# All four sums of a pair's weight blocks made by GpSimd from plain loads

## The chip, the cores and the metric

One core of a Trainium2 chip. Its engines run their own instruction queues side by side: TensorE (PE, multiplies; its weight loads are shown as PEld), VectorE (DVE), ScalarE (ACT), GpSimd (POOL) and SyncE (SP, which issues loads). The metric is the device time of one execution in microseconds. A change of 0.2% (4.5 us) is about what a measurement of this kernel can tell.

## What is computed

A trunk of two layers over 512 tokens of width 1024. Each layer is a half-step SwiGLU, a mixer (attention or convolution), cross attention to a memory and a second half-step SwiGLU. The four SwiGLU blocks are what the change touches:

```python
def swiglu(h, w_in, w_out):
    g, u = split_cols(h @ w_in, (D_FF, D_FF))      # D_FF = 2816
    return (jax.nn.silu(g) * u) @ w_out

x = x + 0.5 * swiglu(rms_norm(x, g[0]), ffn1_w_in[layer], ffn1_w_out[layer])
...
x = x + 0.5 * swiglu(rms_norm(x, g[4]), ffn2_w_in[layer], ffn2_w_out[layer])
```

## The kernel before

All products are fp32 split in two parts, hi and lo (`mm3`: three matmuls for one product). A weight block is loaded (`raw`, or a sum of blocks), ScalarE copies it to the hi part of a tile `w` (in the profile `w<-raw`, `w<-a`, `w<-s`), and VectorE subtracts to get the lo part (the same names on DVE). Six `w` tiles are in use at a time, so splits wait for TensorE to give tiles back.

A feed-forward block has 22 column blocks of 128, done in three parts (`PARTS`: 7, 7 and 8), each followed by its output projection. The first 4 column blocks (5 in the first feed-forward block) are multiplied plainly, with gate and up one after the other. The rest go as *pairs* (`Pair`): the gate block and the up block of one column block, and the two halves of the tokens, are taken as a 2 x 2 block product with seven multiplications in place of eight. The left matrix has the blocks A11 and A12 (`w1`, the gate's columns, first and second half of the contraction: one load of 128 x 1024, tile `raw`, called a1) and A21 and A22 (`w2`, the up columns). Besides A11, A12 and A22 themselves the seven products need four sums of blocks:

- s31, a tile of 1024 columns with A11 + A21 in its left half and A21 + A22 in its right half,
- s2 = A21 + A22 + A11,
- s4 = s2 + A12.

The token side is prepared once a block by VectorE and ScalarE (`Norm.seven`, tiles `hn` and `bop`).

The order of products of a pair on TensorE is: first and second product (from a1), the product with A22 of the pair before it (p4: `w<-a`), the product with s2, the product with s4 of the pair before, and two products from s31, 12 matmuls of 256 columns each. The splits come in the order a1, A22 of the pair before, s2, s4 of the pair before, s31.

Class `Sums` (line 372) makes the sums. `loads` (383) is run through by the loader in the order of the weights: it loads A11 and A22 side by side into a tile of tag P (`s<-ffn_in` on SP), then a1 (`raw<-ffn_in`), then A22 once more by itself (`a<-ffn_in`). `acc` (400) then adds A21 to both halves of the tile by a DMA that accumulates, issued by GpSimd (`s<-ffn_in` on POOL). `add` (406) makes s2 and s4 by two adds on GpSimd (`s<-s,raw`). Buffers: three `raw`, two of tag P, two of tag `ph` (A22), one for s2, two for s4; each has a token that says when it may be used again.

The order on every engine is set ahead of time: tasks are Python generators, and a small planner (`Sched`) with a price for each operation runs the task with the best priority that is ready by its own clock. Its price of the accumulating DMA is 1.04 us and 2.2 us until it is seen; of an add of 512 columns 1.17 us. Waits on tokens come before waits on data, and each engine runs what it is given in order.

Of the kernel before, what the change touches and what calls it, by code (L numbers as in the profile page):

```python
# [9 lines left out]
F32 = mybir.dt.float32  # L10
# [4 lines left out]
ALU = mybir.AluOpType  # L15
# [4 lines left out]
P = 128  # L20
# [27 lines left out]
WMAX = 1024  # L48
# [220 lines left out]
def tile_trunk(ctx: ExitStack, tc: tile.TileContext, a: dict, out: bass.AP, nsteps: int = 8):  # L269
    nc = tc.nc  # L270
    sch = Sched()
    M, SC, TR, OU = ("m", 3), ("s", 2), ("t", 2), ("o", 1)
    pe, act, dve, pool = (Engine(sch, e, n) for e, n in (
        (nc.tensor, "pe"), (nc.scalar, "act"), (nc.vector, "dve"), (nc.gpsimd, "pool")))
    sync, swdge = Engine(sch, nc.sync, "dma"), Engine(sch, nc.gpsimd, "swdge")
# [4 lines left out]
    tp = Pool(sch, ctx.enter_context(tc.tile_pool(name="tmp", bufs=2)), 2)  # L280
# [56 lines left out]
    tok_q, tok_p, tok_pair = Token(2), Token(2), Token(1)  # L337
    tok_slot = Token(9)

    tok_a22, tok_sum = Token(2), Token(2)  # L340


    class Source:


        def __init__(self, tok, uses=1):
            self.tok, self.left = tok, uses
            self.ap, self.ev = None, Event()
# [23 lines left out]
    class Sums:  # L372
# [2 lines left out]


        def __init__(self, w1, w2):
            self.a1 = Chunk(w1, WMAX, 3)
            self.a22, self.s31 = Source(tok_a22), Source(tok_p, 2)
            self.s2, self.s4 = Source(tok_os, 2), Source(tok_sum)  # L380
            self.w1, self.w2 = w1, w2

        def loads(self):
            h = WMAX // 2
            yield tok_p
            t = tp.tile([P, WMAX], F32, tag="P", name="s31")
            t2 = t.rearrange("p (a c) -> p a c", a=2)
            gap = self.w2.offset + h - self.w1.offset
            sync.dma_start(out=t2, in_=bass.AP(self.w1.tensor, self.w1.offset,
                                               [list(self.w1.ap[0]), [gap, 2], [1, h]]))  # L390
            sch.add(self.acc(t, t2), 2)
            yield W.tok_raw
            self.a1.load()
            yield tok_a22
            u = tp.tile([P, h], F32, tag="ph", name="a22")
            sync.dma_start(out=u, in_=self.w2[:, h:])
            self.a22.there(u)
            sch.add(self.add(), 2)

        def acc(self, t, t2):  # L400
            yield Need([t])
            a21 = self.w2[:, :WMAX // 2].unsqueeze(1).to_broadcast([P, 2, WMAX // 2])
            swdge.dma_start(out=t2, in_=a21, accum_op=ALU.add)
            self.s31.there(t)

        def add(self):
            h = WMAX // 2
            yield self.s31.ev
            yield tok_os
            a1, t = self.a1.ap, self.s31.ap  # L410
            yield Need([a1, t])
            s2 = tp.tile([P, h], F32, tag="os", name="s2", bufs=1)
            pool.tensor_tensor(s2, t[:, h:], a1[:, :h], ALU.add)
            self.s31.used()
            self.a1.used()
            self.s2.there(s2)
            yield tok_sum
            s4 = tp.tile([P, h], F32, tag="pl", name="s4")
            pool.tensor_tensor(s4, s2, a1[:, h:], ALU.add)
            self.s2.used()  # L420
            self.a1.used()
            self.s4.there(s4)
# [108 lines left out]
    def token_sums(acc):  # L531

        n = acc.shape[-1] // P
        ps = yield from turn_bank("ss")
        for t in range(n):
            transpose(ps[:, t * P:(t + 1) * P], acc[:, t * P:(t + 1) * P])
        yield Need([ps])
        ss = tp.tile([P, NT], F32, tag="ss", name="ss_c")
        dve.tensor_reduce(ss[:, :n], ps[:, :n * P].rearrange("p (t c) -> p t c", t=n), AX.X, ALU.add)
        tok_t.give()  # L540
        return ss[:, :n]
# [784 lines left out]
    def setup(after):  # L1326
# [79 lines left out]
        for d in range(KD):  # L1406
            raw = tp.tile([P, NMEM], F32, tag="memr", name="mem0")
            swdge.dma_start(out=raw, in_=a["mem"][:, d, :])
            yield Need([raw])
            if d == 0:  # L1410
                act.activation(acc, raw, AF.Square)
            else:
                sq = st[:, 3 + d % 2]
                act.activation(sq, raw, AF.Square)
                yield Need([sq])
                pool.tensor_tensor(acc, acc, sq, ALU.add)
# [621 lines left out]
```

## Time and profile before

| what | us |
|---|---|
| median of 3 runs (2250.31 to 2252.67) | 2251.84 |
| the profiled execution | 2253.21 |
| its span, first to last instruction | 2251.3 |
| TensorE busy | 2213.8 |
| VectorE busy | 1446.7 |
| ScalarE busy | 1073.0 |
| GpSimd busy | 553.3 |
| TensorE's granted clock, mean | 0.998 of full speed |
| read from HBM | 273.18 MB, 123 GB/s over the span |

A row of the order in time has the start, the length, the engine, the source line (nearly always 107, a helper that records every operation), the operation, out<-in, the shape and the count; in brackets stands the engine's idle time before it and what ended it. So instructions are told apart by the names of their tiles. The feed-forward blocks lie at about 9 to 370, 805 to 1158, 1158 to 1511 and 1893 to 2251 us.

### The profile page before, as it was taken

What the parts mean: (1) busy time and instruction counts of PE and PEld (TensorE: products, weight loads), DVE (VectorE), ACT (ScalarE), POOL (GpSimd) and SP (SyncE); (2) the same over time, 40 slices, a digit from 0 to 9 for tenths busy, and PEclk for the clock granted to TensorE, in tenths of its full rate; (3) what the DMA queues carried; (4) which work ended last, traced back from release to release, by engine and by line L of the source; (5) the groups of instructions that cost most, each with busy time, mean ns of one, the idle gap of its engine ahead of it and who ended that gap; (6) DMA issues with size and microseconds to landing.
All of it is one profiled execution on the core that took longest, in us unless ns stands there. A gap on an engine that the chain in (4) does not pass through costs nothing.

```text
span 2251.3 us, 35196 instructions
## 1 busy us (share of the span) xinstructions
PE 2213.8 (98%) x13880; PEld 1979.2 (88%) x13880; DVE 1446.7 (64%) x2302; ACT 1073.0 (48%) x1839; POOL 553.3 (25%) x501
## 2 busy tenths in 40 slices
PE   9998999999999999999999999999999999999999
PEld 7898998889878888999988898989888888889897
DVE  8656565576676686565667474755766667847473
ACT  5344454555565454444544353545544554435352
POOL 1153323432320031313222232323122102213230
PEclk9999999999999999999999999999999999999999
DMA  5455652212332243646534555633123332456562
GB/s 188 117 154 161 166 152 87 75 57 78 102 112 86 93 124 98 171 141 164 147 106 119 153 151 153 170 101 108 58 90 122 98 104 85 131 139 165 144 180 84
DMA packets 106165, 277.59 MB, mean 123 GB/s; under 512 B 11736, under 2 KB 13784, under 8 KB 106000
## 3 DMA queue, kind: packets, MB, share of 16 engines
q1 hardware_dynamic: 83248, 232.63, 31.3%
q0 software_dynamic: 22752, 42.71, 10.8%
q8 instruction: 109, 1.79, 0.3%
q14 instruction: 56, 0.46, 0.1%
HBM read 273.18 MB, written 4.21 MB: 123 GB/s over the span
## 4 chain that ended last, share of the span: by engine, by line
PE 79%; DVE 10%; issue 3%; POOL 3%; DMA 3%; ACT 2%; SPq 0%; POOLq 0%; DVEq 0%; ACTq 0%
PE ps_m L107 44%; PE ps_o L107 27%; DVE w L107 3%; DMA s<-ffn_in 2%; DVE hn L107 2%; PE ps_pv L107 2%; DVE bop L107 2%; PE ps_s L107 1%; PE ps_x L107 1%; PE xo L107 1%; PE ps_pt L107 1%; DVE xl L107 1%; POOL s L107 1%; ACT w L107 1%; POOL qe L107 1%
## 5 line engine op out<-in xcount | busy, mean ns | idle before, releaser
L107 PE MATMUL ps_m<-bop,w 128*128 128x256 f32 x5964 | 728.0, 284 | 17.7 <-DVE g L107 9.2
L107 PEld LDWEIGHTS ps_m<-bop,w 128*128 128x128 f32 x5964 | 722.9, 193 | 23.9 <-DVE g L107 10.2
L107 ACT ACTIVATE w<-raw 128x1024 fp32r<-128x1024 f32 (+2 forms) x332 | 340.4, 1029 | 425.9 <-PE ps_o L107 229.9
L107 DVE TENSOR_TENSOR w<-raw,w 128x1024 fp32r<-128x1024 f32 (+2 forms) x332 | 401.8, 1210 | 148.7 <-ACT w L107 139.2
L107 PE MATMUL ps_m<-xh,w 128*128 128x512 f32 (+1 forms) x1008 | 328.8, 396 | 2.1 <-ACT w L107 2.1
L107 POOL TENSOR_TENSOR s<-s,raw 128x512 f32<-128x512 f32 x142 | 214.5, 1510 | 405.4 <-DMA s<-ffn_in 221.8
L107 PE MATMUL ps_o<-gh,w 128*128 128x512 f32 x944 | 302.5, 389 | 0.0
L107 DVE TENSOR_TENSOR w<-s,w 128x512 fp32r<-128x512 f32 (+1 forms) x213 | 213.7, 1004 | 85.9 <-ACT w L107 57.4
L107 PEld LDWEIGHTS ps_m<-xh,w 128*128 128x128 f32 (+1 forms) x1008 | 188.2, 187 | 44.9 <-ACT w L107 2.7
L107 DVE SCALAR_TENSOR_TENSOR x<-ps_o,x 128x512 f32<-128x512 f32 x160 | 108.6, 687 | 181.5 <-PE ps_o L107 181.2
L107 ACT ACTIVATE w<-s 128x512 fp32r<-128x512 f32 (+1 forms) x213 | 162.5, 767 | 117.6 <-POOL s L107 56.3
L107 PE MATMUL ps_m<-w,xh 128*128 128x256 f32 x1152 | 217.8, 289 | 0.0
L107 PEld LDWEIGHTS ps_o<-gh,w 128*128 128x128 f32 x944 | 177.3, 188 | 36.5
L107 PE MATMUL ps_m<-xl,w 128*128 128x512 f32 (+1 forms) x504 | 197.2, 391 | 0.0
L107 POOL DMA_DIRECT2D s<-ffn_in x71 | 86.1, 1213 | 402.7 <-DMA s<-ffn_in 356.6
L107 PE MATMUL ps_o<-gl,w 128*128 128x512 f32 x472 | 183.8, 389 | 0.0
L107 PEld LDWEIGHTS ps_m<-w,xh 128*128 128x128 f32 x1152 | 178.9, 191 | 1.9 <-issue 1.2
L107 PE MATMUL ps_o<-gated,w 128*128 128x512 f32 x696 | 168.6, 389 | 0.0
L107 PE MATMUL ps_m<-w,xl 128*128 128x256 f32 x576 | 162.7, 282 | 0.0
L107 PEld LDWEIGHTS ps_o<-gated,w 128*128 128x128 f32 x696 | 130.1, 188 | 26.6
L107 POOL TENSOR_TENSOR acc<-acc,sq 128x512 f32<-128x512 f32 x42 | 73.7, 1755 | 246.7 <-ACT sq L107 245.6
L107 PEld LDWEIGHTS ps_m<-xl,w 128*128 128x128 f32 (+1 forms) x504 | 94.5, 187 | 18.7
(453 smaller groups left out, 2812.2 us busy)
## 6 DMA issues: line engine op xcount, KB each, us to landing
raw<-ffn_in SPq DMA_DIRECT2D x103, 512.0 KB, 5.0
s<-ffn_in SPq DMA_DIRECT2D x71, 512.0 KB, 4.3
s<-ffn_in POOLq DMA_DIRECT2D x71, 512.0 KB, 6.0
raw<-ffn_oa SPq DMA_DIRECT2D x64, 448.0 KB, 3.4
a<-ffn_in SPq DMA_DIRECT2D x71, 256.0 KB, 3.8
raw<-ffn_ob SPq DMA_DIRECT2D x32, 512.0 KB, 3.5
raw<-x_kv SPq DMA_DIRECT2D x32, 512.0 KB, 3.4
raw<-even_w SPq DMA_DIRECT2D x24, 512.0 KB, 3.5
```

The lines of the kernel that those rows point to most:

```text
L107: r = fn(*args, **kw)
```

## The change

The accumulating DMA, its task `acc` and the load of A11 and A22 into the tile of s31 are taken out. A21 is loaded by itself, into a buffer of tag `qe` (two of them, used by the attention otherwise), and GpSimd makes all four sums: A21 + A22 into the right half of s31, s2 from it, A21 + A11 into the left half, then s4. The tile of s31 is taken when the adds begin, not when the loads are issued. A22 is now released after the first add and its own split, a1 after three adds and its split.

```diff
@@ class Sums
         def __init__(self, w1, w2):
-            self.a1 = Chunk(w1, WMAX, 3)
-            self.a22, self.s31 = Source(tok_a22), Source(tok_p, 2)
+            self.a1 = Chunk(w1, WMAX, 4)
+            self.a21, self.a22, self.s31 = Source(tok_q, 2), Source(tok_a22, 2), Source(tok_p, 2)
             self.s2, self.s4 = Source(tok_os, 2), Source(tok_sum)
-            self.w1, self.w2 = w1, w2
+            self.w2 = w2
 
         def loads(self):
             h = WMAX // 2
-            yield tok_p
-            t = tp.tile([P, WMAX], F32, tag="P", name="s31")
-            t2 = t.rearrange("p (a c) -> p a c", a=2)
-            gap = self.w2.offset + h - self.w1.offset
-            sync.dma_start(out=t2, in_=bass.AP(self.w1.tensor, self.w1.offset,
-                                               [list(self.w1.ap[0]), [gap, 2], [1, h]]))
-            sch.add(self.acc(t, t2), 2)
             yield W.tok_raw
             self.a1.load()
+            yield tok_q
+            t = tp.tile([P, h], F32, tag="qe", name="a21")
+            sync.dma_start(out=t, in_=self.w2[:, :h])
+            self.a21.there(t)
             yield tok_a22
             u = tp.tile([P, h], F32, tag="ph", name="a22")
             sync.dma_start(out=u, in_=self.w2[:, h:])
             self.a22.there(u)
             sch.add(self.add(), 2)
 
-        def acc(self, t, t2):
-            yield Need([t])
-            a21 = self.w2[:, :WMAX // 2].unsqueeze(1).to_broadcast([P, 2, WMAX // 2])
-            swdge.dma_start(out=t2, in_=a21, accum_op=ALU.add)
-            self.s31.there(t)
-
         def add(self):
             h = WMAX // 2
-            yield self.s31.ev
+            yield tok_p
+            a1, a21, a22 = self.a1.ap, self.a21.ap, self.a22.ap
+            yield Need([a1, a21, a22])
+            t = tp.tile([P, WMAX], F32, tag="P", name="s31")
+            pool.tensor_tensor(t[:, h:], a21, a22, ALU.add)
+            self.a21.used()
+            self.a22.used()
             yield tok_os
-            a1, t = self.a1.ap, self.s31.ap
-            yield Need([a1, t])
             s2 = tp.tile([P, h], F32, tag="os", name="s2", bufs=1)
             pool.tensor_tensor(s2, t[:, h:], a1[:, :h], ALU.add)
             self.s31.used()
             self.a1.used()
             self.s2.there(s2)
+            yield None
+            pool.tensor_tensor(t[:, :h], a21, a1[:, :h], ALU.add)
+            self.a21.used()
+            self.a1.used()
+            self.s31.there(t)
             yield tok_sum
             s4 = tp.tile([P, h], F32, tag="pl", name="s4")
             pool.tensor_tensor(s4, s2, a1[:, h:], ALU.add)
```

GpSimd's queue in the third part of the first feed-forward block, two pairs, before. The sums all have names that begin with s: s_2547 is a tile of s31 (1024 columns), s_2651 an s2, s_2653 an s4.

```order
L107 DMA s_2414<-ffn_in 128x2x512
L107 TENSOR_TENSOR s_2511<-s_2414,raw 128x512
L107 TENSOR_TENSOR s_2517<-s_2511,raw 128x512
L107 DMA s_2547<-ffn_in 128x2x512
L107 TENSOR_TENSOR s_2651<-s_2547,raw 128x512
L107 TENSOR_TENSOR s_2653<-s_2651,raw 128x512
```

The same place of the change; a_2491 and a_2613 are the pair's A21 and A22.

```order
L107 TENSOR_TENSOR s_2672<-a_2491,a_2613 128x512
L107 TENSOR_TENSOR s_2674<-s_2672,raw 128x512
L107 TENSOR_TENSOR s_2672<-a_2491,raw 128x512
L107 TENSOR_TENSOR s_2678<-s_2674,raw 128x512
L107 TENSOR_TENSOR s_2805<-a_2617,a_2746 128x512
L107 TENSOR_TENSOR s_2807<-s_2805,raw 128x512
```

A pair has two adds and a DMA before, and four adds in a row after; nothing else stands between pairs in a run.

SyncE's queue of loads at the start of that part, before, with what each load waits for (DMASW is an accumulating DMA, DMAHW another load, DVE and Pool an engine).

```order
L107 DMA s_2239<-ffn_in 128x2x512 [waits DMASW5_49]
L107 DMA raw<-ffn_in 128x1024 [waits DMAHW5_49,DVE_49]
L107 DMA a_2270<-ffn_in 128x512
L107 DMA s_2272<-ffn_in 128x2x512 [waits DMASW0_49]
L107 DMA raw<-ffn_in 128x1024 [waits DMAHW6_49,DVE_49]
L107 DMA a_2304<-ffn_in 128x512
L107 DMA s_2414<-ffn_in 128x2x512 [waits DMASW4_49,DVE_49,Pool_49]
L107 DMA raw<-ffn_in 128x1024 [waits DMAHW7_49]
L107 DMA a_2465<-ffn_in 128x512 [waits DMAHW2_49,DMAHW0_49,DVE_49]
```

The change, in the second part, where the same holds: the second pair's loads, then those of the third to the fifth.

```order
L107 DMA raw<-ffn_in 128x1024 [waits DMAHW1_49,DVE_49]
L107 DMA a_1055<-ffn_in 128x512
L107 DMA a_1057<-ffn_in 128x512
L107 DMA raw<-ffn_in 128x1024 [waits DMAHW2_49,DVE_49]
L107 DMA a_1095<-ffn_in 128x512 [waits DMAHW4_49,Pool_49]
L107 DMA a_1235<-ffn_in 128x512 [waits DMAHW5_49,DMAHW3_49,DVE_49]
L107 DMA raw<-ffn_in 128x1024 [waits Pool_49]
L107 DMA a_1239<-ffn_in 128x512 [waits DMAHW7_49,Pool_49]
L107 DMA a_1409<-ffn_in 128x512 [waits DMAHW0_49,DMAHW6_49,DVE_49,Activation_49]
L107 DMA raw<-ffn_in 128x1024 [waits Pool_49]
L107 DMA a_1413<-ffn_in 128x512 [waits DMAHW2_49,Pool_49]
L107 DMA a_1545<-ffn_in 128x512 [waits DMAHW3_49,DMAHW1_49,DVE_49]
```

Each pair's three loads are now a1, A21, A22. The first two pairs' A22 wait for nothing; from the third pair on A22 waits for VectorE (the split of A22 two pairs earlier, which shares its buffer), and a1 and A21 of the next pair stand behind it, no longer ahead.

On TensorE, ScalarE and VectorE the order is the same as before, but for a stretch of the first feed-forward block in which the set-up (rotary tables, the memory's norm) is woven into the second part. There, before, the transposes of the memory's squares stand in the run of pairs on TensorE:

```order
L107 MATMUL ps_m<-bop,w 128x256 x474
L107 MATMUL ss<-ident,setup 128x128 x2
L107 MATMUL ps_m<-bop,w 128x256 x90
L107 MATMUL ps_o<-gh_1448,w 128x512
L107 MATMUL ps_o<-gl_1449,w 128x512
```

and now they stand behind the run, in the output projection that follows:

```order
L107 MATMUL ps_o<-gh_2124,w 128x512
L107 MATMUL ps_o<-gh_1484,w 128x512
L107 MATMUL ps_o<-gl_1485,w 128x512
L107 MATMUL ps_o<-gh_1484,w 128x512
L107 MATMUL ss<-ident,setup 128x128 x2
L107 MATMUL ps_o<-gh_1587,w 128x512
```

They moved behind the rest of the run and the first products of the projection.

## The prediction

> **What bounds the kernel now.** I read the page's head, then the stretches of one feed-forward block, then who TensorE waits for, then one pair of weight blocks in order of time. In the head (busy time and share) and the stretch 1277 to 1345 us (span, then each engine's busy time) the reader is to see a TensorE that never rests while pairs are multiplied, and a VectorE (DVE) and GpSimd (POOL) that do.
>
> ```profile
> PE 2213.8 (98%) x13880; PEld 1979.2 (88%) x13880; DVE 1446.7 (64%) x2302; ACT 1073.0 (48%) x1839; POOL 553.3 (25%) x501
> 1277.00:1345.00 68.00, 68.00 (x567) 67.88 (x566) 48.45 (x71) 37.44 (x65) 22.86 (x16) 1.00 0.61 163
> 2123.03 77.87 PE ps_m L107 x648
> ```
>
> The last row, of the chain that ended last, gives 77.87 / 648 = 0.120 us a product; a pair has 84 (seven products of 12), so it takes 10.1 us. Inside a run of pairs there is nothing to gain. What TensorE waits for in sum, times and longest is small:
>
> ```profile
> PE ps_m L107 <- DVE g L107: 9.2, 5, 2.8
> PE ps_m L107 <- DVE w L107: 3.9, 4, 1.0
> PE ps_m L107 <- ACT u L107: 3.3, 3, 2.4
> PE ss L107 <- POOL setup L107: 1.7, 1, 1.7
> ```
>
> These lie at the start of each feed-forward block. An example from the third (order of time; in brackets the idle time and what ended it):
>
> ```profile
> 1206.90 2.32 DVE L107 TENSOR_TENSOR w<-s,w 128x1024 fp32r<-128x1024 f32 x1
> 1209.27 14.41 PE L107 MATMUL ps_m<-bop,w 128*128 128x256 f32 x118 [1.01 <-DVE w L107]
> 1222.51 2.62 POOL L107 TENSOR_TENSOR s<-s,raw 128x512 f32<-128x512 f32 x2 [6.51 <-DMA s<-ffn_in]
> 1226.07 6.20 PE L107 MATMUL ps_m<-bop,w 128*128 128x256 f32 x35 [2.40 <-DVE g L107]
> 874.87 5.35 PE L107 MATMUL ps_m<-bop,w 128*128 128x256 f32 x39 [1.28 <-DVE g L107]
> 1964.04 1.69 PE L107 MATMUL ps_m<-bop,w 128*128 128x256 f32 x12 [1.58 <-DVE g L107]
> ```
>
> The wait at 1226.07 comes from the accumulating DMA: the third pair's sum s2 waits 6.51 us for it, ScalarE's split of s2 waits for that, and behind the split stands the work that frees a PSUM bank. The same wait is 1.28 at 874.87 and 1.58 at 1964.04.
>
> **What the change removes and adds.**
>
> ```profile
> L107 POOL TENSOR_TENSOR s<-s,raw 128x512 f32<-128x512 f32 x142 | 214.5, 1510 | 405.4 <-DMA s<-ffn_in 221.8
> L107 POOL DMA_DIRECT2D s<-ffn_in x71 | 86.1, 1213 | 402.7 <-DMA s<-ffn_in 356.6
> L107 POOL TENSOR_TENSOR s<-s,raw x142: 1266/1359/2359, 53.5 to 2189.4; 128x512 f32<-128x512 f32 x142
> s<-ffn_in POOLq DMA_DIRECT2D x71, 512.0 KB, 6.0
> DMA to landing us min/median/max: 2.5/3.8/8.0
> ```
>
> Each of 71 pairs loses an accumulating DMA (1.21 us of issue on GpSimd, 6.0 us to landing) and the plain load of 512 KB ahead of it, gains a plain load of 256 KB (a21), and GpSimd makes four adds instead of two. An add takes 1.27 us undisturbed (the minimum). GpSimd goes up by 142 x 1.27 - 86 = 94 us, to some 29% of the span: by its share it is no bound. The bytes saved are worth nothing by themselves, since TensorE waits for no plain load of a run of pairs. The last row is of a-loads (256 KB).
>
> The price is in what the adds do to VectorE. One pair in order of time (idle and releaser in brackets):
>
> ```profile
> 1301.46 0.90 DVE L107 TENSOR_TENSOR w<-a,w 128x512 fp32r<-128x512 f32 x1 [0.80 <-ACT w L107]
> 1301.89 1.62 POOL L107 TENSOR_TENSOR s<-s,raw 128x512 f32<-128x512 f32 x1
> 1302.28 0.41 DVE L107 TENSOR_TENSOR g<-ps_m,u 128x256 f32<-128x256 f32 x1
> 1302.39 0.33 SPq L107 DMA_DIRECT2D a<-ffn_in  x1
> 1302.95 1.12 DVE L107 TENSOR_TENSOR w<-s,w 128x512 fp32r<-128x512 f32 x1 [0.25 <-ACT w L107]
> 1303.99 0.41 DVE L107 SCALAR_TENSOR_TENSOR g<-ps_m,g 128x256 f32<-128x256 f32 x1
> 1304.82 0.63 ACT L107 ACTIVATE gh<-g 128x512 fp32r<-128x512 f32 x1 [1.39 <-DVE g L107]
> 1305.48 0.69 DVE L107 TENSOR_TENSOR gl<-g,gh 128x512 fp32r<-128x512 f32 x1 [0.76 <-ACT gh L107]
> 1305.88 0.36 ACT L107 ACTIVATE v__13416<-ps_m 128x256 f32<-128x256 f32 x1
> 1306.09 0.69 DVE L107 TENSOR_TENSOR w<-s,w 128x512 fp32r<-128x512 f32 x1
> 1306.55 0.38 ACT L107 ACTIVATE u<-ps_m 128x256 f32<-128x256 f32 x1 [0.31 <-PE ps_m L107]
> 1308.39 1.22 DVE L107 TENSOR_TENSOR w<-s,w 128x1024 fp32r<-128x1024 f32 x1
> 1309.52 1.22 DVE L107 TENSOR_TENSOR w<-raw,w 128x1024 fp32r<-128x1024 f32 x1
> 1311.18 3.00 POOL L107 TENSOR_TENSOR s<-s,raw 128x512 f32<-128x512 f32 x2 [5.01 <-DMA s<-ffn_in]
> 1311.54 1.49 DVE L107 TENSOR_TENSOR w<-a,w 128x512 fp32r<-128x512 f32 x1 [0.79 <-ACT w L107]
> ```
>
> w<-s of 512 columns takes 0.69 at 1306.09, with no add beside it, and 1.12 at 1302.95, where an add runs until 1303.51 and the split ends 0.56 behind it. w<-a at 1311.54 ends at 1313.03, 0.58 behind the end of an undisturbed add (1311.18 + 1.27 = 1312.45). The second add of that row ends at 1314.18, 1.15 behind the end of w<-a. So a VectorE operation with both inputs in SBUF and an add **take turns**: each stands still until the other is done. g<-ps_m at 1302.28, which reads PSUM, takes 0.41 beside an add: it isn't held up. A turn costs 1.2 for an add, 0.6 for a split of 512 (1305.48 to the next start at 1306.09), 1.1 for one of 1024 (1308.39 to 1309.52).
>
> [...]
>
> Now the sum for a pair in a run. The new adds start when a22 lands, and a22 is loaded when w<-a of two pairs earlier ends (1301.46 + 0.90 = 1302.36, load issued 1302.39): two buffers. So from one w<-a to the next there is a **loop**: the load lands about 2.8 later (from the 2.5 minimum, since nothing is ahead of it in its queue), the first add can start at 3.1. VectorE meanwhile does what stands up to gl: in the trace that ends at 1306.17, 3.8 behind w<-a, of which about 0.65 is waiting for adds that are now elsewhere (w<-s takes 1.12 against 0.69, and waited 0.25 for ScalarE), so 3.15. From there four adds take turns with w<-s (0.6), w<-s (1.1), w<-raw (1.1) and w<-a (0.6): 3.15 + 4 x 1.2 + 3.4 = 11.35. If instead the 512 split slips ahead of the first add, the loop is 3.75 + 3 x 1.2 + 2.8 = 10.15, and its fourth add costs the next loop 1.2 (11.35): 10.75 on average. I take the middle of the two, 11.1: 1.0 over the 10.1 that TensorE needs.
>
> TensorE doesn't feel it at once. u at 1306.55 waited for the pair's first 12 products, so those ended at 1306.5; the product that needs v comes 12 x 0.12 = 1.44 later, at 1307.95, and v was there at 1306.24: 1.6 to spare. With the 0.65 that the chain from w<-a to v gets shorter and 0.2 that w<-a is shorter at first (0.90 against 0.69), 2.4. A block has three runs: 3 pairs (2 in the first), 7 and 8. The first two pairs of a run are loaded ahead (their loads wait for no split in the order of the load queue); 5 and 6 loops remain in the long runs. Stalls: 5 x 1.0 - 2.4 = 2.6 and 6 x 1.0 - 2.4 = 3.6, 6.2 a block, **25 us in four blocks**. With loops of 10.75 and 11.6 (a load of 3.1) it is 10 and 47; a loop of 10.1 gives 0.
>
> At a block's start VectorE is the chain itself (POOL, then DVE, then DVE):
>
> ```profile
> 1187.02 4.04 POOL L107 TENSOR_TENSOR s<-s,raw 128x512 f32<-128x512 f32 x2 [7.06 <-DMA raw<-ffn_in]
> 1187.58 2.33 DVE L107 TENSOR_TENSOR w<-raw,w 128x1024 fp32r<-128x1024 f32 x1
> 1200.39 2.02 DVE bop L107 x2
> ```
>
> The first pair's two adds already hold w<-raw for 1.1 there (2.33 against 1.22). Three more adds (two of the first pair, the first of the second) stand in the same stretch, ahead of the 1.01 wait at 1209.27: 3.6, of which I take 3. Three later blocks: +9. The accumulating DMA's waits go: 2.40 + 1.28 + 1.58 = -5.3, since two adds of 1.27 take the place of 1.21 of issue, 6.0 to landing and one add. Net **+4**. In the first block the rotary and memory set-up shares the stretch; its transposes of the memory's squares move behind the run:
>
> ```profile
> 144.75 16.14 PE L107 MATMUL ps_m<-bop,w 128*128 128x256 f32 x120 [2.44 <-ACT u L107]
> 184.94 1.69 PE L107 MATMUL ps_m<-bop,w 128*128 128x256 f32 x12 [2.79 <-DVE g L107]
> 195.24 0.44 PE L107 MATMUL ss<-ident,setup 128*128 128x128 f32 x2 [1.73 <-POOL setup L107]
> ```
>
> The 2.44, 2.79 and 1.73 may go (-7); but the set-up's adds and DMAs on GpSimd now stand behind four adds a pair, and ScalarE waits for them in order (up to +7). I take 0 and keep both ends.
>
> Sum: 24.8 + 3.7 = +28.5 on the profiled execution's 2253.2 (span 2251.3 and 1.9 around it) = 2281.7; the median of the runs shown is 1.4 lower, so **2280**.
>
> [...]
>
> **The rivals.** (1) Faster: the adds fall where VectorE rests. For it: VectorE is busy 48.45 of 68 us in the run, about 2.9 free a pair, and two more adds are 2.4. If VectorE's lateness stays under 2.4 in every run, the runs cost nothing, the waits of 5.3 go and the first block gains up to 7: 2251.8 - 5 - 5 = 2242. Against it: w<-a is late already with two adds (1.49 at 1311.54), and a held operation holds all behind it. (2) No change: the loop stays near 10.1 because the adds share rather than take turns, and block starts cancel: 2252 to 2255. (3) Worse: loops of 11.6, and ScalarE waiting for the memory's loads in the first block: 47 + 4 + 7 = 2308. (4) That the sums aren't made where the change says isn't possible: the order of instructions shows all of them on GpSimd.
>
> **Chances.** Forecast 0.66 (own range 2262 to 2300), worse 0.11, no change 0.10, faster 0.13. A measurement of this kernel tells about 0.2%, 4.5 us. So slower 0.77, within 0.10, faster 0.13. The range leaves out most of the faster case and the worst: 2249 to 2306.
>
> **What would show it.** Right: w<-a, w<-s and w<-raw longer by about 1.1 in most pairs, adds near 2 us, w<-a spaced about 11 us, TensorE waiting for g or v in each long run from the third or fourth pair. Block starts: 1209.27's wait longer, 1226.07's gone. Wrong: TensorE without a gap in the long runs, that is, w<-a spaced 10.1 although four adds stand between; then adds and VectorE don't meet as I say, or a22 comes earlier than its buffer lets me think.

## The result, and the profile after

| | us |
|---|---|
| before, median of 4 runs (2250.31 to 2255.75) | 2252.26 |
| after, median of 4 runs (2278.31 to 2281.58) | 2280.52 |
| ratio after / before, 95% interval | 1.0126 (1.0114 to 1.0138) |
| profiled execution, before and after | 2253.21, 2280.97 |
| its span, before and after | 2251.3, 2279.2 |

The change makes the kernel 1.26% slower; the forecast was 2280. First the head of the page (busy time and share of the span) and the view of what TensorE waits for (sum, times, longest):

```profile
PE 2231.9 (98%) x13880; PEld 1984.4 (87%) x13880; DVE 1580.4 (69%) x2302; ACT 1071.0 (47%) x1839; POOL 747.3 (33%) x572
PE ps_m L107 <- DVE g L107: 12.2, 19, 5.5
PE ps_m L107 <- DVE w L107: 9.1, 6, 1.9
PE ss L107 <- POOL setup L107: 0.9, 1, 0.9
```

VectorE is 134 us busier with the same 2302 instructions (1580.4 against 1446.7): that is time in which its operations stand still. The splits alone take 121.5 more by their groups; w<-a, for one, takes 1.31 in the mean against 0.84 before, and 0.68 at the least. TensorE waits for g (which VectorE makes from a PSUM bank that is then free again) 19 times instead of 5. GpSimd is busier by 194, of which 71 x 2 adds of 1.27, less the 86 of issue that went, explain 94; the other 100 is again standing still (the third add, s<-a,raw, takes 1.97 in the mean).

Of these 19 waits 16 lie in seven of the long runs of pairs, where there were none; the longest, 5.5, is in the eighth, beside the set-up. TensorE in the run of 7 pairs in the second block, in order of time:

```profile
972.45 1.69 PE L107 MATMUL ps_m<-bop,w 128*128 128x256 f32 x12 [0.39 <-DVE g L107]
974.30 8.90 PE L107 MATMUL ps_m<-bop,w 128*128 128x256 f32 x72 [0.16 <-ACT v__10119 L107]
983.57 1.69 PE L107 MATMUL ps_m<-bop,w 128*128 128x256 f32 x12 [0.37 <-DVE g L107]
985.41 8.89 PE L107 MATMUL ps_m<-bop,w 128*128 128x256 f32 x72 [0.16 <-ACT v__10252 L107]
994.69 9.30 PE L107 MATMUL ps_m<-bop,w 128*128 128x256 f32 x72 [0.39 <-DVE g L107]
```

The pairs are 983.57 - 972.45 = 11.12 and 994.69 - 983.57 = 11.12 apart; 84 products of 0.120 are 10.08. So 1.04 a pair is lost, though the brackets show only 0.39 + 0.16: a row is also longer than its products at each restart (12 products take 1.69 there, and 12 x 0.120 is 1.44). Short waits are read from the spacing, not from the brackets.

Where the 27.9 us of span come from can be read from the start of the same matmul in both traces (counted in order, the first product of each stage; two transposes of the set-up have another place, which makes 0.2 us at most). Differences of after against before, by stage:

| stage | after - before, us |
|---|---|
| seven long runs: 3.6, 3.4, 4.1, 3.1, 3.2, 2.6, 4.1 | +24.0 |
| starts of the second, third and fourth block: 1.7, -1.1, 0.9 | +1.5 |
| start of the first block | +2.7 |
| its run of 7 pairs, beside the set-up | -1.5 |
| all the rest | +1.1 |

One pair of the long run in the third block, VectorE, GpSimd and the load queue in order of time:

```profile
1302.35 1.58 DVE L107 TENSOR_TENSOR w<-s,w 128x1024 fp32r<-128x1024 f32 x1
1302.80 2.28 POOL L107 TENSOR_TENSOR s<-a,raw 128x512 f32<-128x512 f32 x1
1303.85 2.31 DVE L107 TENSOR_TENSOR w<-raw,w 128x1024 fp32r<-128x1024 f32 x1
1305.04 2.28 POOL L107 TENSOR_TENSOR s<-s,raw 128x512 f32<-128x512 f32 x1
1306.09 1.78 DVE L107 TENSOR_TENSOR w<-a,w 128x512 fp32r<-128x512 f32 x1
1307.89 0.33 SPq L107 DMA_DIRECT2D a<-ffn_in  x1
1310.41 0.69 DVE L107 TENSOR_TENSOR gl<-g,gh 128x512 fp32r<-128x512 f32 x1 [0.76 <-ACT gh L107]
1311.02 0.69 DVE L107 TENSOR_TENSOR w<-s,w 128x512 fp32r<-128x512 f32 x1
1311.07 1.80 POOL L107 TENSOR_TENSOR s<-a,a 128x512 f32<-128x512 f32 x1 [3.75 <-DMA a<-ffn_in]
1316.10 1.78 DVE L107 TENSOR_TENSOR w<-a,w 128x512 fp32r<-128x512 f32 x1
```

The reader is to see two things. In these rows, from 1302.80 to 1307.87, the two engines go strictly by turns: each row begins inside the one above and ends 1.1 or 1.2 behind it, w<-a (512 columns) 0.55. And the loop: w<-a ends at 1307.87, the load of the A22 two pairs later is issued at 1307.89, and the first of the next four adds, idle for 3.75, begins when it has landed at 1311.07, 3.2 behind w<-a. In this pair the split of 512 columns got in ahead of that add (1311.02), and the loop is 1316.10 - 1306.09 = 10.01. In the run of 8 pairs of the second block it didn't:

```profile
1092.03 1.78 DVE L107 TENSOR_TENSOR w<-a,w 128x512 fp32r<-128x512 f32 x1
1096.55 1.65 POOL L107 TENSOR_TENSOR s<-a,a 128x512 f32<-128x512 f32 x1 [3.29 <-DMA a<-ffn_in]
1096.97 1.78 DVE L107 TENSOR_TENSOR w<-s,w 128x512 fp32r<-128x512 f32 x1
1103.15 1.78 DVE L107 TENSOR_TENSOR w<-a,w 128x512 fp32r<-128x512 f32 x1
1114.29 1.78 DVE L107 TENSOR_TENSOR w<-a,w 128x512 fp32r<-128x512 f32 x1
```

Here the loops are 11.12 and 11.14. Behind loops of 10.01 comes a longer one (1316.10 to 1328.83, 12.73, in the third block): the fourth add then falls into the next loop (in the third block it starts at 1317.29) and holds a split there.

### The profile page after: what moved, and what is told of

Read it like the earlier page. It is cut to its first block, busy times and chain, and to the rows that moved or that the text cites. A ratio compares the mean times of both kernels' runs of the same rounds, so it can differ in the third digit from the quotient of the medians.

```text
span 2279.2 us, 35116 instructions
## 1 busy us (share of the span) xinstructions
PE 2231.9 (98%) x13880; PEld 1984.4 (87%) x13880; DVE 1580.4 (69%) x2302; ACT 1071.0 (47%) x1839; POOL 747.3 (33%) x572
## 3 DMA queue, kind: packets, MB, share of 16 engines
q8 instruction: 109, 1.79, 0.3%
HBM read 217.34 MB, written 4.21 MB: 97 GB/s over the span
## 4 chain that ended last, share of the span: by engine, by line
PE 69%; DVE 19%; issue 4%; ACT 4%; POOL 2%; DMA 1%; DVEq 0%; SPq 0%; ACTq 0%; POOLq 0%
PE ps_m L107 35%; PE ps_o L107 26%; DVE w L107 10%; DVE hn L107 2%; DVE g L107 2%; PE ps_pv L107 2%; ACT w L107 2%; DVE bop L107 2%; PE ps_s L107 1%; PE ps_x L107 1%; PE xo L107 1%; PE ps_pt L107 1%; DVE xl L107 1%; ACT g L107 1%; DVE gs L107 1%
## 5 line engine op out<-in xcount | busy, mean ns | idle before, releaser
L107 PE MATMUL ps_m<-bop,w 128*128 128x256 f32 x5964 | 740.4, 285 | 21.1 <-DVE g L107 12.2
L107 DVE TENSOR_TENSOR w<-raw,w 128x1024 fp32r<-128x1024 f32 (+2 forms) x332 | 455.7, 1373 | 149.9 <-ACT w L107 142.2
L107 POOL TENSOR_TENSOR s<-a,a 128x512 f32<-128x512 f32 x71 | 105.5, 1486 | 549.2 <-DMA a<-ffn_in 510.8
L107 POOL TENSOR_TENSOR s<-s,raw 128x512 f32<-128x512 f32 x142 | 255.4, 1799 | 89.0 <-issue 74.2
L107 DVE TENSOR_TENSOR w<-s,w 128x512 fp32r<-128x512 f32 (+1 forms) x213 | 248.1, 1167 | 47.1 <-issue 25.9
L107 POOL TENSOR_TENSOR s<-a,raw 128x512 f32<-128x512 f32 x71 | 139.9, 1971 | 0.0
```

The costliest lines, as they stand in the source:

```text
L107: r = fn(*args, **kw)
```

## Experiments

The table above, for each experiment against before (us of one profiled execution each, from the starts of the same matmuls; 40 us into the span, ahead of every pair, these already lie -1.7 to +1.0 from before's, so the columns of the first block are known to a few us only); the last column is the ratio of the timed runs with its interval:

| kernel | A22's buffers | adds on GpSimd | 7 long runs | 3 starts | first start | set-up run | ratio |
|---|---|---|---|---|---|---|---|
| after | 2 | 4 | +24.0 | +1.5 | +2.7 | -1.5 | 1.0126 (1.0114 to 1.0138) |
| e1_s3_memset | 2 | 3 and memsets | -0.9 | -5.6 | +0.9 | -2.3 | 0.996 (0.9946 to 0.9974) |
| e2_a22_three | 3 | 4 | -0.3 | +1.9 | +2.7 | -3.2 | 1.0011 (1.0002 to 1.0021) |
| e4_new_in_runs | 2 | 4 in runs, 2 at starts | +23.6 | +2.3 | 0.0 | -0.7 | 1.0107 (1.0092 to 1.0122) |
| e5_new_at_start | 2 | 4 at starts, 2 in runs | +0.6 | +1.0 | +3.0 | -0.9 | 1.0028 (1.0016 to 1.004) |
| e6_s3_on_vector | 2 | 3 | +15.6 | -3.0 | +2.2 | +0.7 | 1.0076 (1.0063 to 1.0088) |
| e7_three_and_vector | 3 | 3 | -0.9 | -3.5 | +2.7 | -6.5 | 0.9978 (0.9969 to 0.9986) |
| e3_before_two_more | old way | 2 + 2 useless | +68.5 | +13.8 | +3.3 | +4.2 | 1.0414 (1.0397 to 1.0432) |
| e8_before_two_memsets | old way | 2 and memsets | +63.5 | -1.6 | -1.7 | +8.7 | 1.0312 (1.0291 to 1.0333) |

### e1: memsets in place of one add

GpSimd is kept about as long at work. The memsets read nothing, so by the theory that piece holds no operation of VectorE. This kernel leaves A11 + A21 out.

```diff
-            pool.tensor_tensor(t[:, :h], a21, a1[:, :h], ALU.add)
+            pool.memset(t[:, :h], 0.0)
+            pool.memset(t[:, :h], 0.0)
+            pool.memset(t[:, :h // 4], 0.0)
```

> The changed kernel, but the add that makes the left half of s31 is replaced by memsets of that half that take GpSimd about as long (1.2 us) and read nothing: A11 + A21 is left out of the products. Theory (an add that reads SBUF and a VectorE operation with two SBUF inputs take turns): a memset takes no turn, so a loop has three adds instead of four, 11.1 - 1.2 = 9.9, under the 10.1 of TensorE; the stalls of the long runs go, 24 us of the 28, and some of the block starts': about 2255 us. Rival 1 (GpSimd is too slow for four operations in a row): no change, 2280. Rival 2 (it is the late load of A22 alone, behind its two buffers): no change, 2280.

Measured: 2244.46 (2242.8 to 2245.44) beside 2251.33 for before. The long runs lose nothing, as expected; the starts win 5.6, so the time is some 10 below the expected one. VectorE and GpSimd in this kernel, in order of time:

```profile
1302.63 1.30 POOL L107 TENSOR_TENSOR s<-s,raw 128x512 f32<-128x512 f32 x1
1303.26 1.75 DVE L107 TENSOR_TENSOR w<-s,w 128x1024 fp32r<-128x1024 f32 x1
1303.87 1.37 POOL L107 MEMSET s<- 128x512 f32 x3
1304.93 1.21 DVE L107 TENSOR_TENSOR w<-raw,w 128x1024 fp32r<-128x1024 f32 x1
```

The split at 1303.26 waits for the add, which ends at 1303.93, and then runs its 1.1 beside the memsets, to 1305.01; the next one overlaps their end and takes its undisturbed 1.21, against the 2.31 of the same split in the rows of the change. GpSimd's time as such (1.37 for the memsets) is no cost here; the turn is.

### e2: three buffers for A22

The loop is opened, and the four adds stay. In every third pair A22 goes to another tag.

```diff
+            self.tok3, self.tag3, self.bufs3 = (tok_a22, "ph", 2) if len(W.loads) % 3 else (tok_sq, "sq", 3)
-            yield tok_a22
-            u = tp.tile([P, h], F32, tag="ph", name="a22")
+            yield self.tok3
+            u = tp.tile([P, h], F32, tag=self.tag3, name="a22", bufs=self.bufs3)
```

> The changed kernel with A22 in three buffers instead of two (the third from the tag sq, two of whose three buffers are idle in a run), so that the adds of a pair can start up to a pair earlier. Theory: the turns alone fill 4 x 1.2 + 4.9 = 9.7 of 10.1 us; with the 3.1 us of the load's landing out of the loop the adds fall into all of VectorE's time and the stalls of the long runs shrink to a third or less: about 2260 us. Rival 1 (GpSimd's own time, 4 x 1.3 = 5.2 a pair): it had room before, 2280. Rival 2 (the gate of the load alone): all of the long runs' 24 us go, 2256. If the turns weigh by their number alone, whenever they fall, 2280.

Measured: 2253.96 (2252.89 to 2255.06, 10 runs) beside 2251.33. The seven runs lose nothing (-0.3). My theory had some 2260, with up to a third of the stalls left; the time is that of the second rival (the gate of the load alone, 2256). But e1, with two buffers, shows that the gate alone costs the runs nothing either. A group of adds and one of splits over the whole execution (busy, mean ns of one, idle before), then VectorE and GpSimd in order of time:

```profile
L107 POOL TENSOR_TENSOR s<-a,a 128x512 f32<-128x512 f32 x71 | 125.6, 1769 | 436.3 <-DMA a<-ffn_in 386.3 <-DVE w L107 49.9
L107 DVE TENSOR_TENSOR w<-s,w 128x1024 fp32r<-128x1024 f32 x71 | 122.1, 1720 | 27.0 <-issue 26.4 <-ACT w L107 0.5
1309.00 1.94 DVE L107 TENSOR_TENSOR w<-s,w 128x1024 fp32r<-128x1024 f32 x1
1311.02 2.21 POOL L107 TENSOR_TENSOR s<-a,a 128x512 f32<-128x512 f32 x1 [1.16 <-DVE w L107]
```

VectorE is still held: the split of 1024 columns takes 1.72 in the mean (1.21 undisturbed), the first add of a pair 1.77. But the first add at 1311.02 no longer waits for a load; it waits for the split that frees the tile of s31 (1309.00 + 1.94 = 1310.94). So turns that are taken while TensorE has work in hand cost the runs nothing; they cost when the next pair's load hangs on them.

### e3 and e8: before, with GpSimd kept longer

e3 adds two useless adds to before, ahead of the add of s4, with a matching third use of s31:

```diff
+            pool.tensor_tensor(s4, t[:, :h], a1[:, :h], ALU.add)
+            pool.tensor_tensor(s4, t[:, :h], a1[:, :h], ALU.add)
+            self.s31.used()
             pool.tensor_tensor(s4, s2, a1[:, h:], ALU.add)
```

> The kernel before, accumulating DMA and all, with two useless adds of the same size on GpSimd between s2 and s4 of each pair (written to the tile of s4 and then overwritten). Theory: VectorE's work between w<-s (s2) and w<-s (s4) is held twice more, each time up to 1.2 us, and this stretch has 1.6 to spare: 0.3 to 1 us a pair in the long runs, 2265 to 2285. Rival (what cost was the loads' new order and the loss of the accumulating DMA, not the adds): 2252, as before.

Measured: 2346.93 (2341.42 to 2349.18), far above what either theory gave. GpSimd in order of time:

```profile
1355.37 1.20 POOL L107 DMA_DIRECT2D s<-ffn_in  x1
1361.58 5.66 POOL L107 TENSOR_TENSOR s<-s,raw 128x512 f32<-128x512 f32 x4 [5.00 <-DMA s<-ffn_in]
1367.17 1.20 POOL L107 DMA_DIRECT2D s<-ffn_in  x1
```

This kernel has another loop, all of it on GpSimd: issue of the accumulating DMA, 5.00 of waiting for it, four adds, and only then the issue of the next one, 11.80 later. e8 tells it from the held VectorE: memsets in place of the useless adds.

```diff
+            pool.memset(s4, 0.0)
+            pool.memset(s4, 0.0)
+            pool.memset(s4[:, :h // 4], 0.0)
+            pool.memset(s4, 0.0)
+            pool.memset(s4, 0.0)
+            pool.memset(s4[:, :h // 4], 0.0)
             pool.tensor_tensor(s4, s2, a1[:, h:], ALU.add)
```

> The kernel before, with GpSimd kept busy for the time of two more adds a pair ahead of the add that makes s4, by memsets (two of 512 columns and one of 128 for an add), which read nothing. No sum is left out; the s4 tile is written over by the real add. Compared with the run that had two useless adds at that place (+94). Theory (held VectorE operations make most of that): the runs lose little, 2252 to 2265. Rival (GpSimd's queue: the accumulating DMA of the next pair is issued 2.5 later behind the extra work, and that loop of DMA, adds and splits binds): most of the +94 comes back with memsets, 2300 to 2347.

Measured: 2319.81 (2314.76 to 2328.8). The rival is right in the main: with memsets the long runs still lose 63.5 us, beside e3's 68.5. Part of e8's loss is TensorE's clock: the mean granted clock of the profiled execution is 0.989 in e8, 0.996 in e3 and 0.998 before, by estimate 25.5, 9.4 and 4.5 us lost in the whole span (0.011 x 2318.7, 0.004 x 2339.6 and 0.002 x 2251.3); how much of that lies in the long runs these means don't tell. GpSimd in order of time:

```profile
1350.21 1.21 POOL L107 DMA_DIRECT2D s<-ffn_in  x1
1356.03 1.28 POOL L107 TENSOR_TENSOR s<-s,raw 128x512 f32<-128x512 f32 x1 [4.61 <-DMA s<-ffn_in]
1357.26 2.79 POOL L107 MEMSET s<- 128x512 f32 x6
1360.13 1.83 POOL L107 TENSOR_TENSOR s<-s,raw 128x512 f32<-128x512 f32 x1
1361.91 1.20 POOL L107 DMA_DIRECT2D s<-ffn_in  x1
```

The loop is 1361.91 - 1350.21 = 11.70, nearly e3's 11.80. So e3 was no test of turns. It says something of before instead: its GpSimd is busy a quarter of the span, but per pair the accumulating DMA and two adds make a chain of 1.2 + 4.8 + 2.6 = 8.6 out of 10.08. Two more adds would not have fitted beside that DMA, whatever they do to VectorE.

### e4 and e5: the change in the runs alone, at the starts alone

`OldSums` is the class of before, word for word; pi counts the parts of a block from 0.

```diff
-                g = Sums(w_in[j], w_in[NF + j])
+                g = (Sums if pi else OldSums)(w_in[j], w_in[NF + j])      # e4
+                g = (OldSums if pi else Sums)(w_in[j], w_in[NF + j])      # e5
```

> The sums by the old way in the first part of each feed-forward block (the 2 or 3 pairs after the plain ones), by the new way in the second and third. By the comparison of the two traces the long runs carry 22 us of the 28 and the block starts 6: about 2274. If the block starts and the runs depend on one another (a late start saves a stall later), up to 2278 or down to 2270.

> The sums are made the new way only in the first part of each feed-forward block (the run of 2 or 3 pairs); the long runs of 7 and 8 pairs keep the accumulating DMA. Theory (the loss is a loop through A22's two buffers that needs five or six pairs to be felt): the long runs lose nothing, the starts cost what they cost in the full change or a little less, +2 to +4 in all: 2253 to 2257. Rival (the four adds themselves delay every stretch that has them, starts above all): starts at +9 and more, 2261 or above. If starts and runs add up, this and the run with the new way in the long runs alone differ from before by sums that make the full change's +28.

Measured: e4 2276.59 (2275.95 to 2278.36) beside 2251.33, e5 2257.06 (2254.29 to 2257.91) beside 2250.61. The long runs cost 23.6 in e4 and 0.6 in e5. The two losses add up within their intervals: 1.07% + 0.28% against 1.26% for both. e5 is at the upper edge of what was expected; the span of its profiled execution is 2.7 us over before's, its timed median 6.5, so how much the starts cost is known to a few us only.

### e6 and e7: a version that beats both

e6 makes A11 + A21 on VectorE; e7 does that and has e2's three buffers too.

```diff
-            pool.tensor_tensor(t[:, :h], a21, a1[:, :h], ALU.add)
+            dve.tensor_tensor(t[:, :h], a21, a1[:, :h], ALU.add)
```

> The changed kernel with one edit: the third of the four sums, A11 + A21, is made by VectorE in place of GpSimd. All sums are still made, and A22 has two buffers. Theory (VectorE and GpSimd take turns, so an add on GpSimd costs VectorE a turn of 1.2 and the add on VectorE itself costs 0.6 to 0.7): the loop through A22's buffers is about 0.55 shorter, 10.55 to 10.6, stalls per long run of 5 or 6 x 0.5 less the slack of 2.4, that is 0 to 0.6: 2254 to 2258 with the starts. Rival A (turns are no cost; GpSimd's length of four adds before s4 is what counts): GpSimd ends one add earlier, but VectorE has 0.65 more work per pair, the time is that of the change less at most a few us, 2270 or more. Rival B (GpSimd's own queue and turns both vanish with the add, as with the memsets in its place): 2244 to 2248.

Measured: 2267.62 (2265.18 to 2268.6), a miss by some 10 us. VectorE and GpSimd of e6 in order of time:

```profile
1309.03 0.68 DVE L107 TENSOR_TENSOR w<-a,w 128x512 fp32r<-128x512 f32 x1
1319.65 0.68 DVE L107 TENSOR_TENSOR w<-a,w 128x512 fp32r<-128x512 f32 x1
1323.05 1.69 POOL L107 TENSOR_TENSOR s<-a,a 128x512 f32<-128x512 f32 x1 [4.40 <-DMA a<-ffn_in]
1323.49 1.79 DVE L107 TENSOR_TENSOR s<-a,raw 128x512 f32<-128x512 f32 x1
1325.21 1.78 DVE L107 TENSOR_TENSOR w<-s,w 128x512 fp32r<-128x512 f32 x1
1330.56 0.68 DVE L107 TENSOR_TENSOR w<-a,w 128x512 fp32r<-128x512 f32 x1
```

The sum on VectorE isn't the 0.65 I put down: it is held by an add itself (1.79 at 1323.49), and stands ahead of the split of s2 and of what frees the PSUM bank. The loop is 10.62 and 10.91, not 10.55 to 10.6, and each of the seven runs loses about 2.2 (15.6 in all) in place of 0 to 0.6. The direction and the gate (4.40 waiting for the load) are as the theory says, the size of the term isn't.

> The changed kernel with both edits: A22 in three buffers (in every third pair another tag) and the sum A11 + A21 made by VectorE. All sums are made. Theory: the loop no longer binds (nothing to stall in the long runs: 0), and the block starts lose one held turn for each pair there, as with the memsets (-0.5, -3.2, -1.9, and -2.3 in the first block's set-up) less 0.6 for each of the two adds that VectorE makes there: 2245 to 2250, that is faster than before by 0.1 to 0.3%. Rival (VectorE is at its limit at block starts and one more of its own operations costs what the turn cost): same as three buffers alone, 2253 to 2255.

Measured: 2245.28 (2243.64 to 2246.87, 11 runs) beside 2250.61 for before: 0.22% faster (0.14 to 0.31%). From its groups, then VectorE in order of time:

```profile
L107 DVE TENSOR_TENSOR s<-a,raw 128x512 f32<-128x512 f32 x71 | 50.5, 711 | 0.0
1304.14 1.41 DVE L107 TENSOR_TENSOR w<-a,w 128x512 fp32r<-128x512 f32 x1 [0.29 <-ACT w L107]
1314.22 1.41 DVE L107 TENSOR_TENSOR w<-a,w 128x512 fp32r<-128x512 f32 x1 [0.29 <-ACT w L107]
```

w<-a is 10.08 apart, exactly TensorE's pace, and the sum on VectorE now takes 0.71. The gain is at the starts (-3.5) and in the set-up's run (-6.5), where of all waits for g one of 3.8 us is left. These come from one profiled execution each, and that of before (2253.21) lies 2.6 above the median given here: the spans differ by 8.8, the timed medians by 5.3.

## Why the prediction was right, point by point

**The mechanism holds, and both halves of it are needed.** In the pair above splits (2.31 for 1024 columns, 1.21 undisturbed) and adds (2.28, 1.27 undisturbed) take turns, and the loop through A22's two buffers (11.12 against 10.08) makes TensorE wait. Take away one held turn (e1) or the loop (e2) and the long runs lose nothing. The second rival, no change, falls with the time itself, and its sharing with the rows of the pair above (adds of 2.28, in turn with the splits). The rival "faster" was wrong of this change and right of what it would need: with VectorE's lateness kept under the slack, the runs cost nothing, the waits of 5.3 go (shorter ones come at other places; the starts win 3.5) and of the 7 in the first block most. That is e7, 2245 against the 2242 it gave. The sum of the third rival, worse, has a slip: 2251.8 + 47 + 4 + 7 is 2310 and not 2308.

**The loop.** Forecast 11.35 or 10.15, taken as 11.1; measured 11.12 and 10.01, and over the five loops from 1059.24 to 1114.29 in the run of 8 pairs (1114.29 - 1059.24) / 5 = 11.01. The first add came 3.2 behind w<-a (3.1). How often the 512 split slips ahead of the first add I had not worked out: the 11.1 is the middle of two values, and that it came so near is in part luck.

**The runs.** Forecast 2.6 and 3.6; measured 3.4, 3.1 and 2.6 for 7 pairs, 3.6, 4.1, 3.2 and 4.1 for 8. The seven runs come to 22.2 by the forecast, 24.0 measured, 23.6 in e4. Here too luck had a part, since two terms were off and nearly cancel. In the second block's run of 7 the spacings of w<-a are 9.78, 11.12, 11.13, 11.11 and 11.13 (before 9.20, then 10.08 each): four long loops, where I counted five. At the end w<-a is 4.75 later than before and TensorE 3.4, so the slack came to 1.4, where I had 2.4; in the run of 8 it is 5.2 and 4.1, a slack of 1.1. The eighth run is that beside the set-up.

**The starts.** Forecast +9 and -5.3, net +3.7; measured +9.6 up to the first product of the pairs and -8.0 behind it (three blocks together), net +1.5. The place was wrong: the step that failed is "1209.27's wait longer". That wait is gone after. TensorE waits earlier, in the plain products, and the pairs begin without a wait (order of time, TensorE, GpSimd and VectorE):

```profile
1204.33 2.28 POOL L107 TENSOR_TENSOR s<-a,raw 128x512 f32<-128x512 f32 x1
1205.98 3.75 DVE L107 TENSOR_TENSOR bop<-hn,bop 128x512 fp32r<-128x512 f32 x3
1215.66 0.73 PE L107 MATMUL ps_m<-xh,w 128*128 128x512 f32 x2 [1.82 <-DVE w L107]
1222.36 20.78 PE L107 MATMUL ps_m<-bop,w 128*128 128x256 f32 x168
```

The first pair's adds and the first of the second pair come while VectorE prepares the token side (bop, hn) and hold that (these three bop take 3.75 against 2.65 before, two hn at 1210.97 1.97 against 0.87); a split of the last plain block stands behind it on VectorE's queue, and TensorE waits 1.82 for that split in the plain products. In the third block, by the starts of the same matmuls, this wait with what follows it costs 3.7 (forecast 3), the first pair's wait gives back 1.1, and the third pair's (2.40 at 1226.07 before, gone as forecast) gives back 3.9; why more than 1.82 and 2.40 is in the last section. There it is the clock, which the forecast did not have: of the +9.6 about 3.4 are clock (two slow stretches of 3.4 us at 0.50, in the third and fourth block), so the adds themselves cost about 6 where I had 9. That the price came out near 9 was luck.

**The first block.** Forecast a stall of 2.6 in its run of 7 pairs and 0 for the set-up; measured +2.7 at its start, -1.5 in that run and +1.0 ahead of them, +2.2 in all. The three waits listed (2.44, 2.79, 1.73) went or shrank, and one of 5.5 came, the longest in the list of waits. Which of the set-up's operations makes that one I did not try.

**What was worth nothing.** HBM reads fall from 273.18 to 217.34 MB, and nothing of it shows: e2, with the same 217.34 MB and without the loop, is 0.1% slower than before.

In the experiments I was wrong twice: e3's price left out GpSimd's own chain through the accumulating DMA, and e6's left out that the sum moved to VectorE is held in its turn (1.79 at 1323.49).

## What to carry to other kernels

Here an add moved to GpSimd cost VectorE a turn of about 1.1 us where a split stood beside it (w<-a 1.78 against 0.68), and nothing where VectorE read PSUM (g<-ps_m, 0.41 beside an add); but the turns cost the long runs something only where they lay on a loop longer than TensorE's period (11.12 against 10.08: 24.0 us; with the same four adds and the loop open, in e2, -0.3). So look for the loop (buffer freed, load, add, the split that frees it) before counting busy time: here a third buffer for A22 took all 24 us of the long runs back, and with one add given to VectorE the version beats the kernel before. And an engine busy a quarter of the time can have no room, as GpSimd had none before: its queue waited in order for a transfer (5.01 of 10.1 us in the pair shown), and two more adds a pair cost the long runs 68.5 us (e3).

## What the runs showed of the hardware

In the pair shown, from 1302.35 on, both engines have work ready and the turns alternate: neither two adds nor two splits follow each other until 1307.87. In the whole trace of the change no split of 1024 columns takes more than 2.34 (1.21 undisturbed), none of 512 more than 1.81 (0.68) and no add more than 2.36 (1.27), so none was held for a second turn. And two waits on TensorE cost more than themselves here (2.40 about 3.8 and 1.82 about 3.5). The stretch behind such a wait (span, busy times of PE, PEld, DVE, ACT, POOL, granted clock, DMA share, GB/s), before, behind the 2.40 at 1226.07, then after, behind the 1.82 at 1215.66 and one of 1.87 at 856.18:

```profile
1226.10:1229.70 3.60, 3.50 (x20) 3.25 (x21) 2.79 (x6) 3.26 (x6) 0.00 (x0) 0.71 0.41 132
1215.60:1219.20 3.60, 3.54 (x10) 2.82 (x11) 3.50 (x6) 0.00 (x0) 0.00 (x0) 0.61 0.65 216
856.20:859.80 3.60, 3.60 (x16) 2.99 (x17) 3.14 (x5) 0.00 (x0) 0.00 (x0) 1.00 0.70 211
960.00:1000.00 40.00, 38.22 (x306) 36.75 (x305) 36.48 (x43) 21.68 (x38) 22.53 (x12) 1.00 0.28 95
```

The first two stretches cut across the slow time, which lasts 3.4 us at a clock of 0.50: 1227.6 to 1231.0 before, 1216.4 to 1219.8 after. By the starts of the same matmuls TensorE loses 1.4 and 1.7 in it: so the wait of 2.40 was worth about 3.8 and the one of 1.82 about 3.5, nearly all of the 3.9 and 3.7 above. In the fourth block the change has another, 1960.5 to 1963.9, behind a wait of 1.80. Behind the first 15 us and ahead of the end of the program these two executions have two more slow stretches, both in the first block: 145.6 to 149.0 before, 0.8 us behind a wait of 2.44, and 151.4 to 158.3 after, which begins inside the wait of 5.5. All five begin inside a wait of TensorE or up to 1.5 us behind it, and the shortest of these waits is 1.80. But not every such wait has one: behind the 1.87 at 856.18 and the 1.79 at 64.07 after, and behind the 2.79 at 184.94 before, the clock stays at 1.00. What decides it the traces don't show. In the seven long runs neither before nor the change has a slow stretch, so their 24.0 holds none of this: the many waits of under half a microsecond (960 to 1000) leave the clock at 1.00.
